# Expert gathers and their transposes apart, head norms of 1024 tokens at once, and a shorter inverse root

## The chip, the cores and the metric

The kernel runs on one core of a Trainium2 chip. Time is device time in microseconds (us) of one execution; the kernel before has a median of 3851.04 us over 3 runs (3839.18 to 3854.27). Engines are called by the profile's names: PE (TensorE; PEld its weight loads), DVE (VectorE), ACT (ScalarE), POOL (GpSimd), SP (SyncE, which issues most DMAs).

## The reference

One encoder layer on x of 2048 tokens by 1024 channels, in float32:

1. `h = rmsnorm(x) * (1 + sc1) + sh1`, then `p = h @ w_in`, which gives q, k, v for attention (8 query heads, 2 key/value heads of 64) and r, k, v and three low-rank inputs for RWKV-7 (8 heads of 64).
2. Attention: q and k are normalized per head, `y * rsqrt(mean(y*y) + 1e-6) * gain`, rotated, and go through a softmax over all 2048 tokens.
3. RWKV-7 in both directions. Its key `kk` is normalized per head too: `kk / max(sqrt(sum(kk*kk)), 1e-12)`. The output has a group norm per head.
4. `x = x + gt1 * (concat(o_att, o_rwkv) @ w_out)`.
5. Expert choice: `aff = softmax(h2 @ w_router)`; each of 16 experts takes its 256 best tokens, gathers their rows of h2 and computes `(silu(hg @ w_gate) * (hg @ w_up)) @ w_down`, scaled by the affinity, and adds the rows into the output.

## The kernel before, in words

The work is written in Tile: the program names tiles in pools (a tag with n buffers is a ring of n), and a planner orders each engine's instructions. It runs the program on a modelled timeline: when an engine is free there, it issues the earliest instruction of the program that is ready by the model. The order found so is fixed; on the chip each engine takes its own queue in order and waits at semaphores. An instruction can therefore stand in a queue long before its place in the program, and its wait on the chip holds up all behind it on that engine.

Float32 products are made of three single-pass products: each operand is split into a rounded half (ACT) and a remainder (DVE or POOL), `hi*hi + hi*lo + lo*hi` (`split`, L143).

**Projections** (`phase1`, from about 36 to 740 us). Two halves of 1024 tokens. In each, columns of `w_in` are taken 128 at a time (`load_w`, `project`, L245), over four pieces of 256 tokens. `ORDER` fixes the sequence of items: `h` a pair of rwkv heads (three column groups r, k, v, then `prep`), `q` a column group of queries (then `qk_post`), `v` the values, `x` an early load of tokens. Both `qk_post` and `prep` loop over two quarters `q` of 512 tokens and call `head_rsqrt` (L265) in each: ACT squares the tile, four small matmuls with `bones` sum the squares over the 64 rows of each head into PSUM tile `pn` (L272), ACT copies them (`hsm`), PE transposes (L275), DVE scales (`hss`, L280 or L282) and takes the inverse root in 128 x 8 (`rsqrt`, L49 to L61), and splits it into two halves in `rp` (L290, L291); PE transposes back (L292), ACT copies (`hrt`, L294) and four matmuls with `sel` spread the result over the rows again (`pb`, L297). DVE then multiplies it into the tile (`qk_xn` L311, `kkn` L364). `qk_post` also swaps neighbouring rows by two DMAs into `qk_sw`, which shares its one buffer with the squares `qk_sq`. That makes 36 calls of `head_rsqrt`: 2 halves x (5 + 4) column groups x 2 quarters.

The inverse root is a bit trick (L55: shift, L57: subtract from a constant) and three Newton steps of three instructions (L59 to L61), 11 instructions on DVE. The token loads (`load_x`), the group norm of the mixers and the output projection use it as well.

**Mixers** (740 to 2340 us): attention and the RWKV scan side by side. **Output projection** and affinities (2340 to 2590), **router** (2590 to 2657).

**Experts** (`moe`, 2657 to 3850). For each expert: for `f2` = 0 to 3, load and split 256 columns of `w_gate` and `w_up_e` (L1435, L1438); for each of the two column groups `f` of 128 in it, 48 matmuls `gu` (L1496), silu and product `hid` (L1499, L1500), and its split into `dh`, `dl`. Then 96 matmuls `down` (L1515), `y` (L1520), and two scatters that add into the output (POOL, L1521). After `f2` = 0, `choose(e + 1)` prepares the next expert: 16 one-hot tiles `oh` (L1450), 32 small list matmuls into PSUM tile `list_ps` (L1455), the row numbers `idx` (L1459), two gathers of 128 rows into `xg` (POOL, L1460), and at once 16 transposes `moe_tr` in four steps (L1472), each followed by scaling on DVE (`ht`, L1476) and a split into `hh`, `hl`. `list_ps` and `moe_tr` share the PSUM tag `x`, which has two buffers; `idx`, `xg`, `hh` and `hl` have two each.

Of the kernel before, what the change touches and what calls it, by code (L numbers as in the profile page):

```python
# [17 lines left out]
P = 128  # L18
# [19 lines left out]
class Encoder:  # L38
# [10 lines left out]
    def rsqrt(self, pool, y, x, n, pp=P):  # L49

        nc = self.nc
        t = pool.tile([P, n], F32, tag=f"rsq_t{n}", name="rsq_t")
        ti = t.bitcast(I32)
        xi = x.bitcast(I32)
        nc.vector.tensor_scalar(out=ti[:pp], in0=xi, scalar1=1, scalar2=None, op0=ALU.logical_shift_right)  # L55
        yi = y.bitcast(I32)
        nc.vector.tensor_scalar(out=yi, in0=ti[:pp], scalar1=-1.0, scalar2=float(0x5F3759DF), op0=ALU.mult, op1=ALU.add)  # L57
        for _ in range(3):
            nc.vector.tensor_tensor(out=t[:pp], in0=y, in1=y, op=ALU.mult)  # L59
            nc.vector.scalar_tensor_tensor(out=t[:pp], in0=t[:pp], scalar=-0.5, in1=x, op0=ALU.mult, op1=ALU.mult)  # L60
            nc.vector.scalar_tensor_tensor(out=y, in0=t[:pp], scalar=1.5, in1=y, op0=ALU.add, op1=ALU.mult)  # L61


    def params(self):
# [199 lines left out]

    def head_rsqrt(self, sq, scale, eps, floor, kind="n"):  # L265

        nc, tp = self.nc, self.tpool
        tag = kind + "_ps"
        pn = self.ps_n.tile([P, 4, P], F32, tag=tag, name="pn")

        for i in range(4):
            nc.tensor.matmul(pn[32 * i : 32 * i + 32, 0, :], self.bones, sq[:, i * P : (i + 1) * P], start=True, stop=True, tile_position=(0, 32 * i))  # L272
        sm = tp.tile([P, P], F32, tag="hsm", name="hsm")
        nc.scalar.copy(out=sm, in_=pn[:, 0, :])
        nc.tensor.transpose(pn[:, 1, :], sm, self.ident)  # L275
        pv = pn[:, 1, :].rearrange("p (i r) -> p i r", r=32)[:, :, 0:2]
        ss = tp.tile([P, 8], F32, tag="hss", name="hss", bufs=2)
        s3 = ss.rearrange("p (i h) -> p i h", h=2)
        if floor is None:
            nc.vector.tensor_scalar(out=s3, in0=pv, scalar1=scale, scalar2=eps, op0=ALU.mult, op1=ALU.add)  # L280
        else:
            nc.vector.tensor_scalar(out=s3, in0=pv, scalar1=floor, scalar2=None, op0=ALU.max)  # L282
        rn = tp.tile([P, 8], F32, tag="hrn", name="hrn", bufs=2)
        self.rsqrt(tp, rn, ss, 8)

        self.rpn += 1
        rp = self.rp[self.rpn % 2]
        r4 = rp.rearrange("p (i x) -> p i x", x=32)
        r3 = rn.rearrange("p (i h) -> p i h", h=2)
        nc.vector.tensor_copy(out=r4[:, :, 0:2], in_=r3)  # L290
        nc.vector.tensor_tensor(out=r4[:, :, 2:4], in0=r3, in1=r4[:, :, 0:2].bitcast(F32), op=ALU.subtract)  # L291
        nc.tensor.transpose(pn[:, 2, :], rp.bitcast(F32), self.ident)  # L292
        rt = tp.tile([P, P], F32R, tag="hrt", name="hrt")
        nc.scalar.copy(out=rt, in_=pn[:, 2, :])  # L294
        pb = self.ps_n.tile([P, 512], F32, tag=tag, name="pb")
        for i in range(4):
            nc.tensor.matmul(pb[:, i * P : (i + 1) * P], self.sel[:, i, :], rt, start=True, stop=True)  # L297
        return pb

    def qk_post(self, half, j, p, rope):  # L300

        nc = self.nc
        gain = self.qkn[:, 0:1] if j < 4 else self.qkn[:, 1:2]
        co, si = rope
        for q in range(2):
            qs = slice(q * 512, (q + 1) * 512)
            t0 = half * HT + q * 512
            sq, xn, t1, t2 = [self.tpool.tile([P, 512], F32, tag="qk_" + t, name="qk_" + t) for t in ("sq", "xn", "t1", "t2")]
            nc.scalar.activation(out=sq, in_=p[q], func=AF.Square)
            pb = self.head_rsqrt(sq, 1.0 / CH, 1e-6, None, "q")  # L310
            nc.vector.scalar_tensor_tensor(out=xn, in0=p[q], scalar=gain, in1=pb, op0=ALU.mult, op1=ALU.mult)  # L311
            sw = self.tpool.tile([P, 512], F32, tag="qk_sq", name="qk_sw")
            for i in range(2):
                nc.sync.dma_start(out=sw[i : P : 2, :], in_=xn[1 - i : P : 2, :])
            nc.gpsimd.tensor_tensor(out=t1, in0=xn, in1=co[:, qs], op=ALU.mult)
            nc.vector.tensor_tensor(out=t2, in0=sw, in1=si[:, qs], op=ALU.mult)
            nc.vector.tensor_tensor(out=t1, in0=t1, in1=t2, op=ALU.add)
            nc.sync.dma_start(out=self.d_qk[j, :, t0 : t0 + 512], in_=t1)
# [25 lines left out]
    def prep(self, half, ct, rkv, lora, rates, sg):  # L344
# [5 lines left out]
        c2 = lambda ap: ap.rearrange("p (c t) -> p c t", t=P)  # L350
        c3 = lambda ap: ap.rearrange("p (c t) -> p c t", t=CH)
        c4 = lambda ap: ap.rearrange("p (c u t) -> p c u t", u=2, t=CH)
        for q in range(2):
            qs = slice(q * 512, (q + 1) * 512)
            t0 = half * HT + q * 512
# [1 line left out]
            r, k, v = rkv[0][q], rkv[1][q], rkv[2][q]  # L357
            tl = lambda tag, bufs=None: tpool.tile([P, 512], F32, tag=tag, name=tag, bufs=bufs)
            self.to_tokens(v, self.d_v[t0 : t0 + 512, cs_])
            ksq = tl("ksq")  # L360
            act(out=ksq, in_=k, func=AF.Square, scale=self.kk[:, ct : ct + 1])
            pb = self.head_rsqrt(ksq, None, None, 1e-24)
# [59 lines left out]
    def phase1(self):  # L422
# [13 lines left out]
        with ExitStack() as c:  # L436
# [17 lines left out]
            self.rp = [self.tpool.tile([P, P], F32R, name=f"rp{i}") for i in range(2)]  # L454
            self.rpn = 0
            for t in self.rp:
                nc.vector.tensor_copy(out=t, in_=self.zero[:, 0:1].to_broadcast([P, P]))
# [737 lines left out]
class Ffn(Rwkv):  # L1195
# [217 lines left out]
    def moe(self, c):  # L1413
# [27 lines left out]
        def choose(e):  # L1441
# [21 lines left out]
            val = tp.tile([P, 2], F32, tag="val", name="val")  # L1463
            nc.vector.tensor_tensor(out=val, in0=lst[:, :, 3], in1=lst[:, :, 4], op=ALU.add)
            nc.vector.tensor_tensor(out=val, in0=val, in1=lst[:, :, 2], op=ALU.add)
            hh = tp.tile([P, KT, CAP], F32R, tag="hh", name="hh")
            hl = tp.tile([P, KT, CAP], F32R, tag="hl", name="hl")
            for k2 in range(4):
                pt = ps.tile([P, 2, CAP], F32, tag="x", name="moe_tr", bufs=2)
                for i in range(2):  # L1470
                    for h in range(2):
                        nc.tensor.transpose(pt[:, i, h * P : (h + 1) * P], xg[:, h, (2 * k2 + i) * P : (2 * k2 + i + 1) * P], self.ident)  # L1472
                ht = tp.tile([P, 2, CAP], F32, tag="ht", name="ht")
                for i in range(2):
# [4 lines left out]
            return idx, val, hh, hl  # L1479

        def expert(e, st):
            idx, val, hh, hl = st
            nxt = None
            dh = tp.tile([P, 8, CAP], F32R, tag="dh", name="dh", bufs=1)
            dl = tp.tile([P, 8, CAP], F32R, tag="dl", name="dl", bufs=1)
            for f2 in range(4):
# [3 lines left out]
                for i in range(2):  # L1490
                    f = 2 * f2 + i
                    acc = ps.tile([P, 2, CAP], F32, tag="gu", name="gu", bufs=2)
                    for m, (wh, wl) in enumerate((g, u)):
                        for kt in range(KT):
                            for n, (a, b) in enumerate(((wh, hh), (wh, hl), (wl, hh))):
                                nc.tensor.matmul(acc[:, m, :], a[:, kt, i * P : (i + 1) * P], b[:, kt, :],  # L1496
                                                 start=(kt == 0 and n == 0), stop=(kt == KT - 1 and n == 2))
                    hid = tp.tile([P, CAP], F32, tag="hid", name="hid")
                    nc.scalar.activation(out=hid, in_=acc[:, 0, :], func=AF.Silu)  # L1499
                    nc.vector.tensor_tensor(out=hid, in0=acc[:, 1, :], in1=hid, op=ALU.mult)  # L1500
                    self.split(dh[:, f, :], dl[:, f, :], hid)
                if f2 == 0 and e + 1 < NE:
                    nxt = choose(e + 1)
            po = [ps.tile([P, 512], F32, tag=f"d{i}", name="down") for i in range(4)]
            for f2 in range(4):
                w = weight(io["w_down"][0, e, f2 * 256 : (f2 + 1) * 256, :].rearrange("(k p) d -> p k d", p=P))
# [17 lines left out]

        self.listed = None
        st = choose(0)
        for e in range(NE):
            st = expert(e, st)

# [59 lines left out]
```

## Time and profile before

| | us |
|---|---|
| median of 3 runs | 3851.04 |
| profiled execution | 3852.07 |
| its span (first to last instruction) | 3850.1 |
| PE busy | 3546.8 (92%) |
| DVE busy | 2581.8 (67%) |
| ACT busy | 1758.1 (46%) |
| POOL busy | 1537.9 (40%) |

Busy time is the union of an engine's instructions. PE's matmuls are pipelined: one is shown for about 0.28 us, and the next starts 0.11 to 0.12 us after it. PEclk is the granted TensorE clock, 1.00 for 2.4 GHz.

### The profile page before, as it was taken

The numbers are of one execution on the slowest core, as the hardware profiler recorded it, in microseconds if no ns is written. First come the engines' busy times: TensorE is split into PE (matmuls) and PEld (weight loads), VectorE is DVE, ScalarE is ACT, GpSimd is POOL, SyncE is SP. The second block draws the span as 40 slices with busy tenths as digits, with TensorE's granted clock in tenths as the row PEclk, the third lists the DMA queues.
The fourth block names the chain that finished last, engine by engine and source line by source line (L and its number), as shares of the span: only waits on it lengthen the run. The fifth ranks groups of instructions, "written<-read, shape, count | busy, mean of one in ns | idle before, by whom it ended". The sixth has DMA issues, their size and how long they took to land. (4 is left out here: it accounts for less than half of the span.)

```text
span 3850.1 us, 61939 instructions
## 1 busy us (share of the span) xinstructions
PE 3546.8 (92%) x23436; PEld 2875.5 (75%) x23436; DVE 2581.8 (67%) x4704; ACT 1758.1 (46%) x3102; POOL 1537.9 (40%) x1484
## 2 busy tenths in 40 slices
PE   6997898899999999999999998994999999999998
PEld 5986888656666666766666665774888888888897
DVE  6689788886768677558867675457555556555653
ACT  4445444424555555645555663231434443443442
POOL 3344344436363443663363644323223323322331
PEclk8999999789999899999999999996999999999999
DMA  5235334443323433533233233442566667566664
GB/s 182 94 126 167 105 113 137 147 113 78 82 70 90 120 82 82 117 92 85 77 76 92 61 88 113 142 164 99 188 202 202 197 197 211 183 203 200 200 193 134
DMA packets 531230, 510.95 MB, mean 133 GB/s; under 512 B 213304, under 2 KB 449954, under 8 KB 525812
## 3 DMA queue, kind: packets, MB, share of 16 engines
q1 hardware_dynamic: 520612, 472.08, 40.4%
q0 software_dynamic: 10000, 34.91, 4.0%
q8 instruction: 185, 3.03, 0.3%
q14 instruction: 113, 0.93, 0.1%
q10 hardware_dynamic: 320, 0.00, 0.0%
HBM read 392.57 MB, written 109.07 MB: 130 GB/s over the span
## 5 line engine op out<-in xcount | busy, mean ns | idle before, releaser
L1438 DVE TENSOR_TENSOR w_lo<-w_raw,w_hi 128x2048 fp32r<-128x2048 f32 x189 | 462.2, 2451 | 339.2 <-ACT w_hi L1435 339.1
L1496 PE MATMUL gu<-hh,w_hi 128*128 128x256 f32 x2048 | 578.9, 283 | 0.1
L1496 PE MATMUL gu<-hh,w_lo 128*128 128x256 f32 x2048 | 577.4, 282 | 0.0
L1496 PE MATMUL gu<-hl,w_hi 128*128 128x256 f32 x2048 | 575.1, 281 | 0.0
L685 POOL TENSOR_TENSOR acc<-acc,pt 128x512 f32<-128x512 f32 x256 | 363.3, 1424 | 454.8 <-ACT pt L682 433.4
L1435 ACT CAST w_hi<-w_raw 128x2048 fp32r<-128x2048 f32 x192 | 366.8, 1912 | 316.8 <-PE gu L1496 146.1
L682 ACT ACTIVATE pt<-st_ps 128x1024 f32<-128x1024 f32 x256 | 262.2, 1024 | 404.2 <-PE st_ps L681 231.4
L635 DVE TENSOR_REDUCE mx<-s_ps 128x1 f32<-128x512 f32 x512 | 343.3, 681 | 152.8 <-PE s_ps L634 151.0
L245 PE MATMUL proj_ps<-hh,w_hi 128*128 128x258 f32 (+1 forms) x1280 | 375.9, 294 | 28.3 <-DVE s_k L263 12.9
L1496 PEld LDWEIGHTS gu<-hh,w_hi 128*128 128x128 f32 x2048 | 390.1, 191 | 1.6 <-DVE hid L1500 0.2
L1496 PEld LDWEIGHTS gu<-hl,w_hi 128*128 128x128 f32 x2048 | 390.3, 191 | 1.3
L1496 PEld LDWEIGHTS gu<-hh,w_lo 128*128 128x128 f32 x2048 | 390.9, 191 | 0.0
L245 PE MATMUL proj_ps<-hl,w_hi 128*128 128x258 f32 (+1 forms) x1280 | 373.4, 292 | 3.3 <-DVE hl L147 2.5
L245 PE MATMUL proj_ps<-hh,w_lo 128*128 128x258 f32 (+1 forms) x1280 | 372.6, 292 | 0.7 <-POOL w_lo L147 0.7
L147 POOL TENSOR_TENSOR dl<-hid,dh 128x256 fp32r<-128x256 f32 x128 | 139.3, 1089 | 390.1 <-ACT dh L146 389.7
L672 PE MATMUL o_ps<-pt,av 128*64 128x512 f32 x1024 | 279.8, 626 | 6.7 <-ACT pt L682 6.7
L245 PEld LDWEIGHTS proj_ps<-hh,w_hi 128*128 128x128 f32 x1280 | 250.6, 196 | 37.4 <-issue 28.7
L685 DVE TENSOR_TENSOR acc<-acc,pt 128x512 f32<-128x512 f32 x192 | 185.4, 966 | 111.2 <-ACT pt L682 110.6
L245 PEld LDWEIGHTS proj_ps<-hl,w_hi 128*128 128x128 f32 x1280 | 251.3, 196 | 7.3 <-DVE hl L147 2.9
L633 PE MATMUL s_ps<-khh,qhl 128*128 128x512 f32 x512 | 241.5, 473 | 14.7 <-DVE mx L635 12.8
L245 PEld LDWEIGHTS proj_ps<-hh,w_lo 128*128 128x128 f32 x1280 | 250.4, 196 | 4.5 <-issue 2.3
L680 PE MATMUL st_ps<-qhl,khh 128*128 128x512 f32 x512 | 229.1, 447 | 2.6 <-ACT pt L682 2.6
(410 smaller groups left out, 8255.4 us busy)
## 6 DMA issues: line engine op xcount, KB each, us to landing
w_raw<-in_w_gate_dram SPq DMA_DIRECT2D x64, 1024.0 KB
w_raw<-in_w_up_e_dram SPq DMA_DIRECT2D x64, 1024.0 KB
w_raw<-in_w_down_dram SPq DMA_DIRECT2D x64, 1024.0 KB
d_x<-X SPq DMA_DIRECT2D x32, 1024.0 KB
xin<-d_x SPq DMA_DIRECT2D x64, 512.0 KB
w_raw<-in_w_in_dram SPq DMA_DIRECT2D x80, 256.0 KB
mod_w<-in_w_ada_dram SPq DMA_DIRECT2D x64, 256.0 KB
mod_w<-in_w_ada_dram SPq DMA_DIRECT2D x8, 1024.0 KB
```

What stands on the lines that cost most here:

```text
L147: (eng or nc.gpsimd).tensor_tensor(out=lo, in0=src, in1=hi.bitcast(F32), op=ALU.subtract)
L245: nc.tensor.matmul(acc[:, :n], a[:, kt, :], b[:, kt, lo : lo + n], start=(kt == 0 and m == 0), stop=(kt == KT - 1 and m == 2))
L633: nc.tensor.matmul(s, qs[h][:, ts], khh[:, ks], start=True, stop=False)
L635: nc.vector.tensor_reduce(out=mx[:, 4 * h + qt, kc : kc + 1], in_=s, axis=AX.X, op=ALU.max)
L672: nc.tensor.matmul(av[64 * h : 64 * h + 64, :], v[:, kb, :], pt[:, h, :], start=(kb == 0), stop=(kb == 15), tile_position=(0, 64 * h))
L680: nc.tensor.matmul(s[:, h, :], khh[:, ks], qs[h], start=True, stop=False)
L682: nc.scalar.activation(out=pt, in_=s, func=AF.Exp, scale=0.125)
L685: eng.tensor_tensor(out=acc[:, h, :], in0=(first if kb == 1 else acc)[:, h, :], in1=pt[:, h, :], op=ALU.add)
L1435: nc.scalar.copy(out=hi, in_=raw)
L1438: eng.tensor_tensor(out=lo, in0=raw, in1=hi.bitcast(F32), op=ALU.subtract)
L1496: nc.tensor.matmul(acc[:, m, :], a[:, kt, i * P : (i + 1) * P], b[:, kt, :], start=(kt == 0 and n == 0), stop=(kt == KT - 1 and n == 2))
```

## The change

- `rsqrt` computes the same function with 8 instructions. The first makes the start value in one (the integer multiplied by -0.5 and added to the constant), then one step of higher order and one Newton step, with constants folded in.
- `head_rsqrt` takes the squares of 1024 tokens (both quarters) in one tile. The numbers of matmuls and transposes per 512 tokens stay; the copies and the DVE instructions are made once for both quarters, on 16 columns instead of 8. The spreading is a function of its own, `spread`, called per quarter.
- `qk_post` and `prep` square both quarters ahead of their loop. The squares of both have one tag, `sq`, with one buffer of 2 x 512 columns; the swapped tile of `qk_post` is written into it. `hsm` and `hrt` share the tag `hsm`, with one buffer. `rp` has one tile instead of two.
- In `moe`, `choose` ends after the gathers. The transposes are a generator, `fetch`, of four steps; one step stands after each column group of `f2` = 2 and 3.

```diff
     def rsqrt(self, pool, y, x, n, pp=P):
...
+        nc.vector.tensor_scalar(out=y.bitcast(I32), in0=x.bitcast(I32), scalar1=-0.5, scalar2=float(0x5F3759DF), op0=ALU.mult, op1=ALU.add)
+        tt(out=t, in0=y, in1=y, op=ALU.mult)
+        tt(out=t, in0=t, in1=x, op=ALU.mult)
+        stt(out=t, in0=t, scalar=-10.0 / 3.0, in1=t, op0=ALU.add, op1=ALU.mult)
+        stt(out=y, in0=t, scalar=5.0, in1=y, op0=ALU.add, op1=ALU.mult)
+        tt(out=t, in0=y, in1=y, op=ALU.mult)
+        stt(out=t, in0=t, scalar=-0.5 * 0.375**3, in1=x, op0=ALU.mult, op1=ALU.mult)
+        stt(out=y, in0=t, scalar=1.5 * 0.375, in1=y, op0=ALU.add, op1=ALU.mult)
...
     def head_rsqrt(self, sq, scale, eps, floor, kind="n"):
+        pn = self.ps_n.tile([P, 4, P], F32, tag=kind + "_ps", name="pn")
+        for q in range(2):
+            for i in range(4):
+                nc.tensor.matmul(pn[32 * i : 32 * i + 32, q, :], self.bones, sq[:, q, i * P : (i + 1) * P], start=True, stop=True, tile_position=(0, 32 * i))
+        sm = tp.tile([P, 2, P], F32, tag="hsm", name="hsm")
+        nc.scalar.copy(out=sm, in_=pn[:, 0:2, :])
+        for q in range(2):
+            nc.tensor.transpose(pn[:, 2 + q, :], sm[:, q, :], self.ident)
...
+        for q in range(2):
+            nc.tensor.transpose(pn[:, q, :], rp[:, q, :].bitcast(F32), self.ident)
+        rt = tp.tile([P, 2, P], F32R, tag="hsm", name="hrt")
+        nc.scalar.copy(out=rt, in_=pn[:, 0:2, :])
+        return rt
+
+    def spread(self, rt, q, kind="n"):
+        pb = self.ps_n.tile([P, 512], F32, tag=kind + "_ps", name="pb")
         for i in range(4):
-            nc.tensor.matmul(pb[:, i * P : (i + 1) * P], self.sel[:, i, :], rt, start=True, stop=True)
+            self.nc.tensor.matmul(pb[:, i * P : (i + 1) * P], self.sel[:, i, :], rt[:, q, :], start=True, stop=True)
         return pb
...
     def prep(self, half, ct, rkv, lora, rates, sg):
+        ksq = tpool.tile([P, 2, 512], F32, tag="sq", name="ksq")
+        for q in range(2):
+            act(out=ksq[:, q, :], in_=rkv[1][q], func=AF.Square, scale=self.kk[:, ct : ct + 1])
+        rt = self.head_rsqrt(ksq, None, None, 1e-24)
         for q in range(2):
...
+            pb = self.spread(rt, q)
...
         def choose(e):
...
+            return [idx, val, xg]
+
+        def fetch(st):
+            xg = st[2]
             hh = tp.tile([P, KT, CAP], F32R, tag="hh", name="hh")
             hl = tp.tile([P, KT, CAP], F32R, tag="hl", name="hl")
+            st[2:] = hh, hl
             for k2 in range(4):
...
+                yield
 
         def expert(e, st):
...
+                    if f2 >= 2:
+                        next(steps, None)
                 if f2 == 0 and e + 1 < NE:
                     nxt = choose(e + 1)
+                    steps = fetch(nxt)
```

## Rows read from the trace of the kernel before

**Rows 1.** The page's first part: busy us, share of the span, instructions.
```profile
PE 3546.8 (92%) x23436; PEld 2875.5 (75%) x23436; DVE 2581.8 (67%) x4704; ACT 1758.1 (46%) x3102; POOL 1537.9 (40%) x1484
```

**Rows 2.** Busy time by stage: stretch, length, busy of PE, PEld, DVE, ACT, POOL, PEclk.
```profile
140.00:740.00 600.00, 528.34 (x4000) 483.49 (x3998) 510.49 (x1085) 292.46 (x625) 260.77 (x188) 0.95 0.39 129
2657.00:3767.00 1110.00, 1054.84 (x7928) 984.77 (x7927) 636.76 (x796) 463.48 (x484) 328.54 (x242) 0.99 0.63 197
...
3030.00:3104.00 74.00, 69.81 (x530) 64.98 (x530) 43.04 (x55) 30.83 (x32) 22.64 (x16) 1.00 0.64 200
3767.00:3834.00 67.00, 67.00 (x481) 63.05 (x480) 29.15 (x24) 24.96 (x26) 11.94 (x11) 1.00 0.42 126
```

**Rows 3.** PE's waits, 2660 to 3850 us: total us, times, longest.
```profile
PE moe_tr L1472 <- DMA xg<-d_xh,idx: 41.1, 23, 4.5
PE list_ps L1455 <- DVE ht L1476: 13.9, 11, 1.3
```

**Rows 4.** PE's waits in the projections, 140 to 740 us.
```profile
PE pbo L410 <- DVE pinv L408: 15.1, 6, 4.8
PE proj_ps L245 <- DVE s_k L263: 12.9, 5, 3.9
...
PE proj_ps L245 <- DVE s_r L263: 6.3, 3, 2.8
PE pn L292 <- DVE rp L291: 5.8, 6, 2.6
PE pn L272 <- ACT qk_sq L309: 5.3, 4, 3.4
PE proj_ps L245 <- DVE s_v L263: 4.0, 2, 3.4
PE pn L272 <- DVE kkn L364: 2.9, 4, 1.9
```

**Rows 5.** PE's timeline in the sixth expert: start, duration, instruction, [idle before].
```profile
3030.28 0.28 PE L1496 MATMUL gu<-hh,w_hi 128*128 128x256 f32 x1
...
3046.53 0.30 PE L1472 MATMUL moe_tr<-ident,xg 128*128 128x128 f32 x1 [1.81 <-DMA xg<-d_xh,idx]
...
3054.64 0.88 PE L1472 MATMUL moe_tr<-ident,xg 128*128 128x128 f32 x6 [1.08 <-DMA xg<-d_xh,idx]
...
3064.65 0.56 PE L1455 MATMUL list_ps<-parts,oh 128*128 128x5 bf16 x16 [1.30 <-DVE ht L1476]
```

**Rows 6.** POOL's timeline in the same expert.
```profile
3039.81 1.00 POOL L1460 DMA_INDIRECT xg<-d_xh,idx  x1 [0.30 <-issue]
...
3044.63 3.04 POOL L1460 DMA_INDIRECT xg<-d_xh,idx  x1 [0.92 <-DVE oh L1450]
...
3056.95 1.30 POOL L147 TENSOR_TENSOR hl<-ht,hh 128x512 fp32r<-128x512 f32 x1 [4.63 <-ACT hh L146]
```

**Rows 7.** DVE by line, 0 to 830 us: count, busy us, mean ns, idle before.
```profile
L59 DVE TENSOR_TENSOR rsq_t<-hrn 128x8 f32<-128x8 f32 x108 | 32.8, 304 | 2.3
...
L60 DVE SCALAR_TENSOR_TENSOR rsq_t<-rsq_t,hss 128x8 f32<-128x8 f32 x108 | 25.7, 238 | 2.4
L61 DVE SCALAR_TENSOR_TENSOR hrn<-rsq_t,hrn 128x8 f32<-128x8 f32 x108 | 25.6, 237 | 2.3
...
L55 DVE TENSOR_SCALAR rsq_t<-hss 128x8 int32<-128x8 int32 x36 | 14.5, 403 | 0.4
L57 DVE TENSOR_SCALAR hrn<-rsq_t 128x8 int32<-128x8 int32 x36 | 13.5, 376 | 0.4
```

**Rows 8.** Line 59 alone: ns min/median/max, first and last start, forms.
```profile
L59 DVE TENSOR_TENSOR rsq_t<-hrn x108: 141/166/1286, 72.4 to 775.5; 128x8 f32<-128x8 f32 x108
...
L59 DVE TENSOR_TENSOR rsq_t<-gn_m x33: 129/161/2258, 1187.9 to 2343.9; 128x16 f32<-128x16 f32 x21, 128x4 f32<-128x4 f32 x12
```

**Rows 9.** ACT's timeline at the head of one norm's chain.
```profile
421.25 0.63 ACT L309 ACTIVATE qk_sq<-p 128x512 f32<-128x512 f32 x1 [0.95 <-DVE qk_t L316]
```

**Rows 10.** PE's timeline at the end of the same chain.
```profile
434.86 0.56 PE L297 MATMUL pb<-hrt,sel 128*128 128x128 f32 x4
```

More of the change, by code (lines that the diff above doesn't have):

```diff
@@ L51, in rsqrt @@
         nc = self.nc
[L52 to L61, printed above, removed]
+        t = pool.tile([P, n], F32, tag=f"rsq_t{n}", name="rsq_t")[:pp]
+        tt, stt = nc.vector.tensor_tensor, nc.vector.scalar_tensor_tensor
+        nc.vector.tensor_scalar(out=y.bitcast(I32), in0=x.bitcast(I32), scalar1=-0.5, scalar2=float(0x5F3759DF), op0=ALU.mult, op1=ALU.add)
[6 more added lines that the diff above has]
+        stt(out=y, in0=t, scalar=1.5 * 0.375, in1=y, op0=ALU.add, op1=ALU.mult)
     def params(self):
@@ L267, in head_rsqrt @@
         nc, tp = self.nc, self.tpool
[L268 to L277, printed above, removed]
+        pn = self.ps_n.tile([P, 4, P], F32, tag=kind + "_ps", name="pn")
[6 more added lines that the diff above has]
+            nc.tensor.transpose(pn[:, 2 + q, :], sm[:, q, :], self.ident)
+        pv = pn[:, 2:4, :].rearrange("p q (i r) -> p (q i) r", r=32)[:, :, 0:2]
+        ss = tp.tile([P, 16], F32, tag="hss", name="hss", bufs=2)
         s3 = ss.rearrange("p (i h) -> p i h", h=2)
@@ L282, in head_rsqrt @@
             nc.vector.tensor_scalar(out=s3, in0=pv, scalar1=floor, scalar2=None, op0=ALU.max)
-        rn = tp.tile([P, 8], F32, tag="hrn", name="hrn", bufs=2)
-        self.rsqrt(tp, rn, ss, 8)
+        rn = tp.tile([P, 16], F32, tag="hrn", name="hrn", bufs=2)
+        self.rsqrt(tp, rn, ss, 16)
         self.rpn += 1
-        rp = self.rp[self.rpn % 2]
-        r4 = rp.rearrange("p (i x) -> p i x", x=32)
+        rp = self.rp[self.rpn % len(self.rp)]
+        r4 = rp.rearrange("p q (i x) -> p (q i) x", x=32)
         r3 = rn.rearrange("p (i h) -> p i h", h=2)
@@ L291, in head_rsqrt @@
         nc.vector.tensor_tensor(out=r4[:, :, 2:4], in0=r3, in1=r4[:, :, 0:2].bitcast(F32), op=ALU.subtract)
[L292 to L295, printed above, removed]
+        for q in range(2):
[5 more added lines that the diff above has]
+        pb = self.ps_n.tile([P, 512], F32, tag=kind + "_ps", name="pb")
         for i in range(4):
-            nc.tensor.matmul(pb[:, i * P : (i + 1) * P], self.sel[:, i, :], rt, start=True, stop=True)
+            self.nc.tensor.matmul(pb[:, i * P : (i + 1) * P], self.sel[:, i, :], rt[:, q, :], start=True, stop=True)
         return pb
@@ L304, in qk_post @@
         co, si = rope
+        sq = self.tpool.tile([P, 2, 512], F32, tag="sq", name="qk_sq")
+        for q in range(2):
+            nc.scalar.activation(out=sq[:, q, :], in_=p[q], func=AF.Square)
+        rt = self.head_rsqrt(sq, 1.0 / CH, 1e-6, None, "q")
         for q in range(2):
@@ L307, in qk_post @@
             t0 = half * HT + q * 512
-            sq, xn, t1, t2 = [self.tpool.tile([P, 512], F32, tag="qk_" + t, name="qk_" + t) for t in ("sq", "xn", "t1", "t2")]
-            nc.scalar.activation(out=sq, in_=p[q], func=AF.Square)
-            pb = self.head_rsqrt(sq, 1.0 / CH, 1e-6, None, "q")
+            xn, t1, t2 = [self.tpool.tile([P, 512], F32, tag="qk_" + t, name="qk_" + t) for t in ("xn", "t1", "t2")]
+            sw = sq[:, q, :]
+            pb = self.spread(rt, q, "q")
             nc.vector.scalar_tensor_tensor(out=xn, in0=p[q], scalar=gain, in1=pb, op0=ALU.mult, op1=ALU.mult)
-            sw = self.tpool.tile([P, 512], F32, tag="qk_sq", name="qk_sw")
             for i in range(2):
@@ L352, in prep @@
         c4 = lambda ap: ap.rearrange("p (c u t) -> p c u t", u=2, t=CH)
+        ksq = tpool.tile([P, 2, 512], F32, tag="sq", name="ksq")
+        for q in range(2):
+            act(out=ksq[:, q, :], in_=rkv[1][q], func=AF.Square, scale=self.kk[:, ct : ct + 1])
+        rt = self.head_rsqrt(ksq, None, None, 1e-24)
         for q in range(2):
@@ L359, in prep @@
             self.to_tokens(v, self.d_v[t0 : t0 + 512, cs_])
-            ksq = tl("ksq")
-            act(out=ksq, in_=k, func=AF.Square, scale=self.kk[:, ct : ct + 1])
-            pb = self.head_rsqrt(ksq, None, None, 1e-24)
+            pb = self.spread(rt, q)
             kk = tl("kkn", 2)
@@ L453, in phase1 @@
                 nc.vector.memset(self.bones[64 * h : 64 * h + 64, h : h + 1], 1.0)
-            self.rp = [self.tpool.tile([P, P], F32R, name=f"rp{i}") for i in range(2)]
+            self.rp = [self.tpool.tile([P, 2, P], F32R, name=f"rp{i}") for i in range(1)]
             self.rpn = 0
             for t in self.rp:
-                nc.vector.tensor_copy(out=t, in_=self.zero[:, 0:1].to_broadcast([P, P]))
+                nc.vector.tensor_copy(out=t, in_=self.zero[:, 0:1].unsqueeze(2).to_broadcast([P, 2, P]))
             self.sel = self.tpool.tile([P, 4, P], F32R, name="sel")
@@ L1478, in choose @@
                 self.split(hh[:, 2 * k2 : 2 * k2 + 2, :], hl[:, 2 * k2 : 2 * k2 + 2, :], ht)
-            return idx, val, hh, hl
+                yield
         def expert(e, st):
             idx, val, hh, hl = st
-            nxt = None
+            nxt, steps = None, iter(())
             dh = tp.tile([P, 8, CAP], F32R, tag="dh", name="dh", bufs=1)
@@ L1526, in moe @@
         st = choose(0)
+        for _ in fetch(st):
+            pass
         for e in range(NE):
```

## The prediction

> **What bounds the kernel now.** I read the page's busy shares first: TensorE is busy 92% of the span, VectorE 67%, ScalarE 46%, GpSimd 40% [rows 1]. The table of stages comes next, because the change touches only some of them [rows 2]. It shows the projections (140 to 740 us; the first 140 us are the start) with TensorE busy 528 of 600 us and VectorE 510, so two engines are nearly full there; and fifteen of the sixteen experts (2657 to 3767 us) with TensorE busy 1055 of 1110 and VectorE at 637, so TensorE alone sets the pace. The mixers between them and the output projection run the edited inverse root a few times only. So what can be won is TensorE's idle time: 72 us in the projections, 55 us in the experts. The third view, the waits of TensorE, names what ends it. In the experts there are only two causes: 41.1 us in 23 waits of the transposes `moe_tr` for the gathered rows `xg`, and 13.9 us in 11 waits of the list matmuls for VectorE's `ht` [rows 3]. In the projections the causes are many and small, and most are VectorE's [rows 4].
>
> An expert without a successor has none of this: the sixteenth takes 67 us with TensorE busy throughout, while the sixth, which chooses the seventh, takes 74 with 69.8 busy [rows 2].
>
> **Experts: the waits for the gathers.** The transposes stand in TensorE's queue at the place where the planner thinks that the rows have landed, and TensorE takes its queue in order. In the sixth expert, which starts at 3030.28, the first transpose comes at 3046.53 after 1.81 us of idleness and the next six at 3054.64 after 1.08 us, both ended by the DMA [rows 5]. The two gathers were issued at 3039.81 and 3044.63 [rows 6], so the second half of the rows is there 24.4 us after the expert's start.
>
> Where does the change put the first transposes? Behind the fifth of eight column groups. The sixteenth expert gives the pitch: 384 narrow matmuls and 96 of double width in 67.0 us are 576 units of 0.116 us, so a group of 48 takes 5.6 us and five take 28 [rows 2]. 28 is later than 24.4, by 3.6 us, and each further step of four transposes comes 5.6 us later. If the queue keeps this order, the 41.1 us go almost whole. What is late next is the list matmuls' wait: they take a PSUM buffer that a transpose's reader `ht` has to free. Today eight transposes come nearly together and their readers stand behind weight splits on VectorE; the sixth expert loses 1.30 us there [rows 5]. With steps 5.6 us apart the buffer should mostly be free, but the next list can also land behind another weight split, so I take half: 7 us of 13.9, between nothing and all of it.
>
> What the move carries with it: per expert 16 transposes, 8 VectorE scalings, 4 ScalarE copies and 4 GpSimd subtractions of 1.3 us each [rows 6]. None is added; all run some 12 us later. VectorE has 31 of 74 us free in an expert, ScalarE 43, GpSimd 51 [rows 2]. The last step is issued after the eighth group, at about 46 us, and its result is needed at the next expert's start, behind 96 down matmuls (22 us); if that cover were gone the next expert's first matmuls would wait. The gathers themselves and the scatters ahead of them on GpSimd's queue keep their places; the four subtractions now come before the next scatter, which waits for the down matmuls anyway. SP's weight loads are not passed. So this part gives 41 + 7 = 48 us; the bounds are 0 (the planner pulls the transposes forward again) and 61 (all 55 us, and some 6 of the 11 us that a granted clock of 0.99 over 1110 us costs [rows 2]).
>
> **Projections: norms of 1024 tokens at once.** There are 36 calls of the norm now and 18 after. Each call's inverse root is 11 VectorE instructions now and 8 after: 396 become 144, so 252 go. In the trace the 396 took 32.8 + 25.7 + 25.6 + 14.5 + 13.5 = 112 us, 283 ns each [rows 7]. Their median is 166 ns for 8 columns, and 161 for the 16-column form that the group norm uses [rows 8], so the doubled width is free. Saved on VectorE: 252 x 0.166 = 42 us at the least, 252 x 0.283 = 71 us at the most. Three smaller instructions around each root (scale, copy, subtract) go with the 18 calls too; I leave them as a margin. TensorE's work stays: the same four sums, one transpose there, one back and four spreads for each 512 tokens. ScalarE's two copies become half as many, twice as wide, which costs nothing on an engine that is half idle in this stage [rows 2].
>
> Here a rule speaks against the upper figure. The rows show single small instructions far above their median (up to 1.29 us) [rows 8]. The Trainium skill, page "SBUF — State Buffer", section "SBUF: two separate sides", says that VectorE and GpSimd lock a shared port pair for a whole instruction and that the other engine blocks fully. By it a stall behind GpSimd does not vanish with the instruction that met it but falls on the next one with two SBUF inputs; the saving would then be the 42 us and not the 71. The long single instructions agree with it; that a stall is passed on, no row of before shows.
>
> How much of 42 to 71 us reaches the end? TensorE's waits for VectorE here are 15.1 + 12.9 + 6.3 + 5.8 + 4.0 + 2.9 = 47 us [rows 4]. Between none and all of that I take a bit over a third, 18 us: VectorE's load of 510 us falls by about a tenth, and the waits for the chain's own steps (`rp`, `kkn`, 8.7 us together) occur half as often.
>
> What is added is a dependency. The first 512 tokens' normalized tile now waits for the sums of all 1024. In program order it costs little, since the projections of r, k and v of a head are all issued before its norms. But `sq` and `hsm` have one buffer each and are now shared by the q/k norms and the rwkv norms; `hsm` holds the result until the second half has been spread. Behind a late `hsm` copy, ScalarE's evictions of the projections would queue, and behind these TensorE's accumulators. That is a rival below. Against it stands one gain that I don't price: the second half's Square today waits for the swapped tile of the first half to be read [rows 9], and no longer does.
>
> **Inverse root elsewhere.** The output projection and the group norm lose 3 small instructions per call beside a busier TensorE. Only the start (first x tile) and the last token tile before the router lie open: 2 x 3 x 0.17 = 1 us. Bounds 0 and 3. The order of the mixers is planned anew, since everything before them moves; I allow 10 us either way.
>
> **Sum.** 48 + 18 + 1 = 67 us, from the profiled execution's 3852.1 us (span 3850.1 and 2 us around it): 3785. That execution lies 1 us above the median of the three runs, 3851.0, so nothing is to be corrected.
>
> **The rivals.**
> - *The planner undoes the move.* List matmuls of the eighth expert, which stand in the program after a quarter of the seventh, run at 3064.65, in the middle of the sixth [rows 5]. So the planner fills what it takes for idle time with later work, and could issue the transposes as early as before. For: that row. Against: they now stand behind all of groups three to five in priority, and those are ready whenever their weights are. The experts give 5 us or so, the rest as above: 3852 - 5 - 18 - 1 = 3828.
> - *Waits for gathers go, the projections give nothing.* VectorE's 42 us end up as its own idle time because the waits are for chains across engines. 3852 - 48 = 3804.
> - *Both give more.* 61 in the experts and 40 of the 47 in the projections: 3751.
> - *Slower: the joint norms lie bare.* One chain from Square to spread lasts 421.25 to 434.86, 13.6 us [rows 9, 10]. If a third of the 18 joint chains stood bare because of the single `hsm` or `sq` buffer, TensorE would lose 6 x 13.6 = 82 us: 3852 - 49 + 82 = 3885. The total turns slower when four of 18 are bare (54 us against 49). Against it: today the waits for the chain's own steps (5.3 + 5.8 + 2.9 = 14 us, [rows 4]) are 3% of 36 chains of 13.6 us; they are well covered by projections.
>
> **How the numbers follow.** Forecast 45%; projections give nothing 25%; planner undoes the move 13%; both give more 10%; slower 7%. The range 3742 to 3830 takes in the forecast, both smaller gains and most of the larger one, and leaves out the slower case. What this kernel's measurement can tell from no change is about 0.5%, 19 us: faster means below 3832, slower above 3870. Faster: nearly all of the first two and of "more", about half of the third, 80%. Same: the rest of the third, and mishaps of the planner's new order in the others, 13%. Slower 7%.
>
> **What would show it.** Experts: the wait of `moe_tr` for `xg` near 0 in the table of TensorE's waits, and an expert at about 70.5 us instead of 74. Still 30 us or more there: the planner pulled them forward. List waits: at or below 7 us; above 14, the PSUM buffer is the new bound. Projections: 18 norms, VectorE busy 40 to 70 us less between 140 and 740 us, the stage about 18 us shorter. A stage that is not shorter although VectorE is less busy speaks for the second case; new waits of TensorE for `hsm` or the sums, or of ScalarE for them, for the slower one. The prediction is wrong if the experts' part stays within 20 us of before, or if the projections get longer.

## The result, and the profile after

The changed kernel takes 3744.51 us (median of 4 runs, 3741.77 to 3751.49) against 3846.84 us for the kernel before on the same chips (3839.18 to 3854.27): a ratio of 0.9737, 95% interval 0.9711 to 0.9762, about 102 us less. The forecast was 67 us less (3785, range 3742 to 3830). The profiled execution took 3751.5 us, 7 above its median, as the one of before stood some 5 above the median that more runs gave it.

Stages, from the first start of a mixer matmul (`p`), of the output projection, of the first `gu`, and the end of the last `down` in the two traces:

| us | start and projections | mixers | output projection, router | experts |
|---|---|---|---|---|
| before | 739 | 1597 | 322 | 1177 |
| after | 724 | 1576 | 326 | 1108 |
| difference | -15 | -21 | +4 | -69 |

The page's first line after the change; it answers to [rows 1].

```profile
PE 3509.9 (94%) x23436; PEld 2856.7 (76%) x23436; DVE 2516.7 (67%) x4289; ACT 1755.2 (47%) x3066; POOL 1512.5 (40%) x1484
```

Busy time by stage after, with the columns of [rows 2]: projections, mixers, the experts with a successor, the sixth of them, the sixteenth.

```profile
140.00:724.00 584.00, 521.18 (x3968) 479.80 (x3966) 475.87 (x789) 289.49 (x595) 265.76 (x188) 0.94 0.39 133
724.00:2300.00 1576.00, 1515.03 (x8963) 1047.22 (x8964) 1142.01 (x1913) 838.00 (x1666) 768.43 (x859) 0.96 0.36 90
2626.00:3668.00 1042.00, 1042.00 (x7923) 978.61 (x7923) 617.81 (x795) 464.09 (x483) 306.30 (x242) 1.00 0.66 209
2974.00:3044.00 70.00, 70.00 (x532) 65.67 (x531) 42.13 (x55) 30.88 (x32) 20.28 (x16) 1.00 0.67 211
3668.00:3734.00 66.00, 66.00 (x483) 61.80 (x482) 29.65 (x24) 25.00 (x26) 12.14 (x11) 1.00 0.43 128
```

In the experts TensorE is busy 1042 of 1042 us at a granted clock of 1.00, where it was 1055 of 1110 at 0.99. Both waits of [rows 3] are gone: the table of TensorE's waits has no row at all between 2626 and 3749 us. The transposes of the sixth expert (which starts at 2974.55) on TensorE's timeline, to be laid beside [rows 5]; no idle time stands behind them. They run in two bursts of eight, 26.3 and 38.4 us after the start, and not in four steps of four:

```profile
3000.80 1.03 PE L1492 MATMUL moe_tr<-ident,xg 128*128 128x128 f32 x8
3012.98 1.03 PE L1492 MATMUL moe_tr<-ident,xg 128*128 128x128 f32 x8
```

And its gathers on GpSimd's timeline, beside [rows 6]:

```profile
2987.64 3.04 POOL L1474 DMA_INDIRECT xg<-d_xh,idx  x1 [3.32 <-DVE idx L1473]
2990.98 1.07 POOL L1474 DMA_INDIRECT xg<-d_xh,idx  x1 [0.30 <-issue]
```

They go out 13.1 and 16.4 us after the expert's start and not 9.5 and 14.4 as before. The list matmuls ahead of them moved too: before, sixteen of them ran half an expert early (34 us into the expert ahead, [rows 5]), now nearly all run 11 and 15 us into the expert in which the program has them:

```profile
2985.45 0.53 PE L1469 MATMUL list_ps<-parts,oh 128*128 128x5 bf16 x15
2989.58 0.56 PE L1469 MATMUL list_ps<-parts,oh 128*128 128x5 bf16 x16
```

I read the reason from the trace: the last transposes hold the two PSUM buffers until 39 us into the expert, so the next list is no longer pulled so far ahead. The second gather lands 23.3 us after the expert's start (24.3 before), 3.0 us ahead of the first transposes.

### The profile page after: what moved, and what is told of

It reads as the page before. It is cut to its first block, busy times and chain, and to the rows that moved or that the text cites. A ratio compares the mean times of both kernels' runs of the same rounds, so it can differ in the third digit from the quotient of the medians.

```text
span 3749.8 us, 61495 instructions
## 1 busy us (share of the span) xinstructions
PE 3509.9 (94%) x23436; PEld 2856.7 (76%) x23436; DVE 2516.7 (67%) x4289; ACT 1755.2 (47%) x3066; POOL 1512.5 (40%) x1484
## 3 DMA queue, kind: packets, MB, share of 16 engines
q1 hardware_dynamic: 520612, 472.08, 41.1%
## 5 line engine op out<-in xcount | busy, mean ns | idle before, releaser
L1452 DVE TENSOR_TENSOR w_lo<-w_raw,w_hi 128x2048 fp32r<-128x2048 f32 x189 | 432.3, 2293 | 385.8 <-ACT w_hi L1449 385.4
L699 POOL TENSOR_TENSOR acc<-acc,pt 128x512 f32<-128x512 f32 x256 | 354.9, 1391 | 469.0 <-ACT pt L696 456.0
L696 ACT ACTIVATE pt<-st_ps 128x1024 f32<-128x1024 f32 x256 | 262.2, 1024 | 394.8 <-PE st_ps L695 221.2
L699 DVE TENSOR_TENSOR acc<-acc,pt 128x512 f32<-128x512 f32 x192 | 194.7, 1014 | 91.0 <-ACT pt L696 90.3
```

Of the source, the lines that this page charges most:

```text
L696: nc.scalar.activation(out=pt, in_=s, func=AF.Exp, scale=0.125)
L699: eng.tensor_tensor(out=acc[:, h, :], in0=(first if kb == 1 else acc)[:, h, :], in1=pt[:, h, :], op=ALU.add)
L1452: eng.tensor_tensor(out=lo, in0=raw, in1=hi.bitcast(F32), op=ALU.subtract)
```

## The experiments

Medians against the kernel before, run beside each; stages from the profiles as above.

| run | ratio (95%) | start and projections | mixers | out, router | experts |
|---|---|---|---|---|---|
| changed_again | 0.9757 (0.9730 to 0.9784) | 724 | 1574 | 325 | 1108 |
| experts_only | 0.9818 (0.9796 to 0.9841) | 734 | 1583 | 320 | 1108 |
| norms_root | 0.9901 (0.9876 to 0.9926) | 722 | 1578 | 325 | 1173 |
| norms_only | 1.0016 (0.9994 to 1.0038) | 737 | 1607 | 321 | 1168 |
| root_only | 1.0024 (1.0007 to 1.0041) | 732 | 1595 | 325 | 1173 |
| tokens_later | 0.9918 (0.9892 to 0.9943) | 722 | 1572 | 325 | 1178 |
| old_root_heads | 0.9870 (0.9816 to 0.9924) | 733 | 1619 | 325 | 1108 |
| spare_three | 0.9758 (0.9702 to 0.9814) | 720 | 1573 | 325 | 1109 |
| old_root_after | 0.9775 (0.9734 to 0.9816) | 722 | 1600 | 321 | 1108 |
| old_root_after_again | 0.9775 (0.9750 to 0.9800) | 722 | 1601 | 320 | 1107 |
| steps_early | 0.9811 (0.9765 to 0.9858) | 720 | 1582 | 324 | 1122 |
| steps_burst | 0.9803 (0.9758 to 0.9848) | 724 | 1587 | 325 | 1121 |

**The four parts.** Each part of the diff alone, or two together; no other edit.

> The kernel before with the change in the experts alone; projections, mixers and output projection keep their old order. Theory (the experts' gain is the waits of TensorE for gathers and list buffers, 55 us, plus the clock that these waits cost, some 10): 65 to 70 us faster than before, every expert that has a successor at 69 to 70 us, and the mixers unchanged within 5 us, with the stretches of half clock near 1284 and 1345 us there again. Rival A (the 21 us in the mixers differ from execution to execution): the mixers are about 20 us shorter here too, 85 to 90 us in all. Rival B (the experts gain only beside the rest of the change, for instance because their weights start earlier): below 50 us.

70 us faster, experts 1177 to 1108, no wait of TensorE in them. The gain is the theory's, B is refuted; the mixers were to stay within 5 us and did not. A holds in part: the order of TensorE, ScalarE and GpSimd ahead of the experts is that of before, and yet the mixers of this execution are 14 us shorter than those of the execution of before. The stretch of half clock near 1284 us, which the theory expected again, is not there: the granted clock from 1280 to 1320 us is 0.91, and was 0.62 before. First before, then experts_only:

```profile
739.00:2336.00 1597.00, 1533.41 (x8975) 1056.53 (x8974) 1145.51 (x1961) 842.69 (x1675) 777.90 (x861) 0.95 0.36 90
```

```profile
734.00:2317.00 1583.00, 1518.96 (x8974) 1047.97 (x8975) 1149.51 (x1961) 841.35 (x1675) 779.74 (x860) 0.96 0.36 90
```

TensorE's idle time is the same (64 us); the granted clock is not. So a difference of some 15 us in one pair of profiles of the mixers proves nothing. The -15 and -21 us of the first table are -10 and -7 if experts_only, which has before's order there, stands for before.

> The kernel before with the inverse root of 8 instructions alone, 36 calls as before. Theory (an inverse root is hidden work; it takes 108 VectorE instructions out of the projections, 18 to 31 us of VectorE's time there, and some 5 of it reach TensorE): projections 0 to 8 us shorter, the mixers anywhere within 20 us either way because they are planned anew, in all 0 to 25 us faster. Rival C (the mixers gain 21 us because their group norms' roots are shorter): mixers 15 to 25 us shorter, with VectorE's waits there shorter and not the clock. Rival D (the roots' length sets the projections): projections 12 us shorter or more by this alone.

> The kernel before with the norms of 1024 tokens at once, but the old inverse root of 11 instructions, and the old experts. Theory (half as many chains is what the projections gain from): projections 8 to 14 us shorter than before, VectorE busy some 50 us less between 140 and 740 us; mixers planned anew, within 20 us either way. Rival D (the root's length sets the projections): projections 0 to 4 us shorter. Rival E (the single buffers for the squares and the copies cost what the fewer chains give): projections not shorter, with new waits for hsm.

> The changed kernel with the old experts; everything ahead of the experts stands as in the changed kernel. Theory: 30 to 36 us faster than before, of which 12 to 15 in the projections and about 20 in the mixers, with less half clock between 1280 and 1360 us than before; with the experts' 65 to 70 us it makes up the whole 102. Rival A (the mixers' part differs from execution to execution): 12 to 16 us faster only. Rival F (part of the experts' gain comes through the parts ahead of them): the two parts do not add up to 102, by more than 10 us.

Neither norms nor root gains anything alone; both are slightly slower if anything (norms +6 us, root +9 us, by the ratios). Together they gain 38 us (28 to 48). With the experts' 70 that is 108, and the whole was measured at 101 and 93 by its two ratios: the parts add up within their intervals. How the 38 divide between projections and mixers single profiles don't settle. D falls with root_only, whose projections are 7 us shorter and not 12. E falls in its simple form: TensorE waits for `hsm` 1.9 us in all in norms_only. My own theories fall too. root_only was to be up to 25 us faster; and norms_only has 198 VectorE instructions fewer than before in the roots alone (36 x 11 against 18 x 11), VectorE is busy 481 us in its projections and not 510, and they are not shorter (737) than before's 734 to 739.

**Load, length or order?** Three edits on the changed kernel ask which of them matters. The old root in the head norms alone:

```diff
-        self.rsqrt(tp, rn, ss, 16)
+        self.rsqrt_old(tp, rn, ss, 16)
```

> The changed kernel with the old root of 11 instructions in the 18 joint head norms alone, 54 VectorE instructions more in the projections than the changed kernel; the new root everywhere else. Theory (the joint norms win in the projections only together with the shorter root, through the order that the planner then finds): projections 592 to 600 us instead of 584, the mixers as in the changed kernel, in all 10 to 20 us slower than it, about 3760. Rival C (the shorter roots of the group norms are what the mixers gain from): mixers near 1577 us too; so the mixers decide between C and a mere by-product of the projections' plan, under which they are at 1590 or more and the whole at 3770 to 3785. Rival J (VectorE's load alone counts): 54 instructions of 0.17 to 0.28 us are 9 to 15 us of VectorE's time, at its 80% load 2 to 5 us in all, about 3748.

The same 54 instructions more, but beside the chain:

```diff
         self.rsqrt(tp, rn, ss, 16)
+        for _ in range(3):
+            spare = tp.tile([P, 16], F32, tag="hss", name="spare", bufs=2)
+            nc.vector.tensor_tensor(out=spare, in0=self.sparein[:, 0:16], in1=self.sparein[:, 0:16], op=ALU.mult)
...
+            self.sparein = self.tpool.tile([P, 16], F32, name="sparein")
+            nc.vector.memset(self.sparein, 1.0)
```

> The changed kernel with three more small VectorE instructions (128 x 16, on tiles that nothing needs) beside each of the 18 joint head norms, off its chain: the load of the old root without its latency. Theory (the order that the planner finds, and not the load or the chain's length, makes the difference): a new order, and a time that may lie anywhere between that of the changed kernel and 20 us more. Rival J (VectorE's load): within 6 us of the run with the old root in the heads. Rival K (the length of the chain): within 5 us of the changed kernel, projections 580 to 586 us.

Beside the chain the load costs nothing that can be told: spare_three's ratio is 0.9758, the changed kernel's 0.9737 and 0.9757. The same load inside the chain costs 47 us (medians 3800 against 3753, run beside each other); in the profiles, of which spare_three's lies 9 us below its median, 13 us of the difference lie in the projections and 46 in the mixers, where these norms run only in the first 16 us. Projections and mixers of spare_three, then of old_root_heads:

```profile
140.00:720.00 580.00, 521.69 (x3965) 480.98 (x3963) 473.39 (x834) 289.24 (x593) 263.77 (x188) 0.94 0.39 134
720.00:2293.00 1573.00, 1511.03 (x8966) 1041.91 (x8966) 1142.92 (x1917) 841.57 (x1670) 772.65 (x860) 0.96 0.36 91
```

```profile
140.00:733.00 593.00, 524.33 (x3969) 480.24 (x3969) 475.92 (x840) 288.92 (x591) 260.98 (x188) 0.95 0.38 131
733.00:2352.00 1619.00, 1541.80 (x8966) 1061.13 (x8966) 1140.06 (x1914) 840.30 (x1670) 774.92 (x860) 0.94 0.35 88
```

VectorE is busy as long in both, so J falls. In the mixers both run the same number of matmuls; what differs is their sequence. Compared by name, TensorE's sequence in the mixers is the changed kernel's in spare_three, without one difference; in old_root_heads it differs in over 200 places. norms_only runs nearly the sequence of old_root_heads there (27 places differ) and takes 1607 us. So the longer mixers come with the other order that the planner finds once the chain in the projections is longer. How much of the 46 us that order causes is open: TensorE's idle time accounts for 15, and the lower granted clock for some 28 (an estimate from the length and the mean clock of the two stretches, 0.943 against 0.959). Before and experts_only show that some 15 of such clock can come and go under one order.

The rest of the forecasts did less well. For old_root_heads the whole (3800) lies above both that it named, 3760 and 3770 to 3785. In spare_three the new order that my theory awaited hardly came (25 places of TensorE's in the projections, none in the mixers); rival K's forecast for the projections, 580 to 586, came true with 580. In the projections, then, the chain's length and the order that comes with it are not told apart.

The old root where the head norms are not:

```diff
-        self.rsqrt(self.r_p, st, sv, 2 * nt)
+        self.rsqrt_old(self.r_p, st, sv, 2 * nt)
...
-                self.rsqrt(tp, rs, ss[:, 0:1], 1)
+                self.rsqrt_old(tp, rs, ss[:, 0:1], 1)
```

> The changed kernel with the old root of 11 instructions in the group norms of the mixers and in the output projection, the new one in the projections. Theory (the mixers' gain is a by-product of the new plan and of the clock, not of shorter roots there): the same as the changed kernel within 12 us, mixers within 10 us of 1576. Rival C (the shorter roots of the group norms are it): mixers 15 to 25 us longer, 1590 to 1600 us.

> The changed kernel itself, beside the next run on one chip, so that the two can be compared; nothing is edited. Expected: 0.974 of the time of before, about 3745 us, mixers 1570 to 1590 us.

> The changed kernel with the old root in the group norms and the output projection, once more, because its first interval overlapped that of the changed kernel; the mixers' order on all engines is that of the changed kernel up to 1971 us, with 14 differences on TensorE after it. Theory (under one order the length of the group norms' roots is worth little): within 8 us of the run beside it. Rival C (the shorter roots of the group norms are a good part of the mixers' gain): 12 to 25 us slower than the run beside it, mixers 1590 to 1605 us.

The mixers are 1600 and 1601 us long in the two profiles, where C had them, against 1572 to 1587 in the seven others with the new root and the joint norms, all of which run one TensorE order there; the output projection is 4 us shorter. But both profiled executions were the slowest of their runs, 6 and 14 us above the median. The medians of the second comparison are 3753.9 against 3743.6, between the two forecasts (within 8, 12 to 25), and the intervals overlap. Rival C is neither confirmed nor refuted: by my estimate from these numbers 0 to 20 us of the mixers may go with the group norms' roots, though root_only has these roots too and no shorter mixers (1595). It stays open.

An edit that was to make a new order did not:

```diff
-            self.to_tokens(v, self.d_v[t0 : t0 + 512, cs_])
             pb = self.spread(rt, q)
             kk = tl("kkn", 2)
             stt(out=kk, in0=k, scalar=self.kkh[:, ct : ct + 1], in1=pb, op0=ALU.mult, op1=ALU.mult)
+            self.to_tokens(v, self.d_v[t0 : t0 + 512, cs_])
```

> The changed kernel with the old experts (as the run norms_root), in which the transposes and the store of v stand behind the key's product instead of ahead of the spread: the same instructions, another order in the program. Theory (norms and root together win 36 us partly because their plan happens to leave less half clock and fewer late instructions): the time differs from norms_root by more than its scatter, by 8 to 30 us, most of it in the projections and mixers. Rival I (the 36 us belong to the 306 instructions that are gone from VectorE): within 6 us of norms_root.

It is 6 us from norms_root. But TensorE's sequence in the projections and in the mixers is the same as there, so this run tells the two expectations apart in nothing.

**Where the transposes stand.** Two edits of the place, on the changed kernel:

```diff
-                    if f2 >= 2:
+                    if 2 <= f < 6:
                         next(steps, None)
```

> The changed kernel with the four steps of transposes behind the third to sixth column group instead of the fifth to eighth. Theory (what the move wins is that the transposes stand behind the landing of the gathers, which is about 24 us after an expert's start in both kernels): the third group ends near 17 us, so TensorE waits for the second half of the rows again, 2 to 7 us in each of 15 experts, and the stage of the experts is 30 to 80 us longer than in the changed kernel. Rival G (the win is the spreading over four places, wherever they are): the experts as fast as in the changed kernel, within 10 us. Rival H (the planner decides where they stand, and the place in the program matters little): within 10 us too, with the transposes still issued at 26 us or later.

```diff
-                    if f2 >= 2:
-                        next(steps, None)
+                    if f == 4:
+                        for _ in steps:
+                            pass
```

> The changed kernel with all four steps together behind the fifth column group. Theory (late is what counts; spreading only keeps the list matmuls from waiting for a PSUM buffer): no wait for the gathers, at most 1.3 us per expert for a buffer, so the experts 0 to 20 us longer than in the changed kernel. Rival G (spreading is what counts): 30 us longer or more.

TensorE's waits over the experts, steps_early and then steps_burst:

```profile
PE moe_tr L1492 <- DMA xg<-d_xh,idx: 13.1, 8, 2.2
```

```profile
PE moe_tr L1492 <- DMA xg<-d_xh,idx: 17.6, 14, 2.1
PE moe_tr L1492 <- DVE ht L1496: 0.5, 1, 0.5
```

Both are 13 to 14 us slower in the experts, and in both the wait for the gathers is back in part. For steps_early that is less than the 30 us of the theory and more than the 10 of rivals G and H: all three missed. Its gathers go out 13.1 and 16.4 us into the sixth expert (start 2981.2) as in the changed kernel, but its first transpose is due before the first of them has landed:

```profile
3003.67 0.30 PE L1492 MATMUL moe_tr<-ident,xg 128*128 128x128 f32 x1 [1.48 <-DMA xg<-d_xh,idx]
```

For steps_burst the theory's 0 to 20 us holds and G's 30 falls, though there was to be no wait for the gathers. steps_burst shows the rival of the prediction at work: the program places the first transpose behind the fifth group, and it is issued in the third, 16 us into the sixth expert (start 2986.7):

```profile
3002.68 0.30 PE L1492 MATMUL moe_tr<-ident,xg 128*128 128x128 f32 x1 [1.43 <-DMA xg<-d_xh,idx]
...
3013.86 0.82 PE L1492 MATMUL moe_tr<-ident,xg 128*128 128x128 f32 x6
3018.84 0.60 PE L1492 MATMUL moe_tr<-ident,xg 128*128 128x128 f32 x4
```

So place alone does not hold them back. With steps spread to the eighth group, the PSUM buffers are taken longer, list and gathers follow later, and the planner, which issues a transpose when its model takes the rows for landed, does so at 26 us. That the buffers are the link is read from the traces and was not tried by itself.

## Why the prediction was right, and where not

- *Waits for the gathers, 41 us:* right; they went whole, and experts_only shows that this edit alone does it. The margin was right (3.6 us forecast, 3.0 in the sixth expert), the way to it in part luck: the queue did not keep the program's order (two bursts at 26.3 and 38.4 us and not four steps from 28 us on), and the gathers, which were to keep their places, went out 2 to 4 us later. The rival of the undone move did not come true in this kernel, but does in part in steps_burst.
- *List buffers, 7 of 13.9 us:* undersized; all went. With the clock (about 23 us at half clock in the experts before, 3 after: some 10 us) that makes 41.1 + 13.9 + 10 = 65 of the 69 us measured, where the prediction had 48 and an upper bound of 61. Of the rest, 1.5 us is the sixteenth expert's (last section); some 2 are not assigned.
- *Projections, 18 us:* 15 measured in this pair of profiles, 10 against experts_only, and for a wrong reason. TensorE's idle time up to the first mixer matmul falls by 8 us (101 and 102 in the two executions of before's order, 94 and 93 in the two of the changed kernel); the rest is matmul time, and experts_only, with before's order, has 6 us less of that too, at a higher granted clock. The step that failed is "VectorE's load of 510 us falls by about a tenth, and the waits for the chain's own steps (`rp`, `kkn`, 8.7 us together) occur half as often", as a reason for 18 us. The chain's own waits did shrink (8.7 to 3.0 us), but the accumulators' waits grew from 23 to 25 us (`s_k`, `s_r`, `s_v`, [rows 4]), and all waits for VectorE together fell only from 52 to 48. norms_only and spare_three show that VectorE's load alone decides nothing here: with 29 us less of it the stage was 2 us shorter, 54 instructions more beside the chain did not lengthen it. TensorE's waits in the projections after:

```profile
PE proj_ps L247 <- DVE s_k L265: 23.8, 8, 4.8
PE pbo L424 <- DVE pinv L422: 7.9, 7, 2.7
...
PE pn L297 <- DVE rp L295: 1.1, 3, 0.6
...
PE proj_ps L247 <- DVE s_v L265: 0.8, 2, 0.6
```

- *The saving on VectorE, 42 to 71 us:* right for the roots, wrong for the engine. The head norms' roots took 112 us in 396 instructions before [rows 7] and take 53 us in 144 after, 59 less. That is under the upper figure because those left are slower each, 367 ns on average against 283, with medians almost as before (164 to 176 ns by line against 166). The small instructions around the roots fell too, from 24 to 11 us. Yet VectorE's busy time between 140 us and the first mixer matmul fell from 510 to 476 only, 34 us, which is below the lower end. Most of the difference was taken up by the 304 instructions of `prep`, which are the same in both kernels and rose from 285 to 311 us; the rest is not assigned. Three lines of the roots (VectorE by line, 0 to 830 us, the columns of [rows 7]), then one line of `prep` before and after:

```profile
L56 DVE TENSOR_TENSOR rsq_t<-hrn 128x16 f32<-128x16 f32 x18 | 8.6, 479 | 0.6
L61 DVE TENSOR_TENSOR rsq_t<-hrn 128x16 f32<-128x16 f32 x18 | 7.5, 414 | 0.1
L55 DVE TENSOR_SCALAR hrn<-hss 128x16 int32<-128x16 int32 x18 | 7.4, 411 | 0.4
```

```profile
L399 DVE SCALAR_TENSOR_TENSOR a<-a,kkn 128x512 f32<-128x512 f32 x32 | 30.6, 957 | 0.7 <-ACT kd L398 0.3
```

```profile
L413 DVE SCALAR_TENSOR_TENSOR a<-a,kkn 128x512 f32<-128x512 f32 x32 | 40.4, 1261 | 0.0
```

  The longest root instruction after shows a stall: on VectorE's timeline it lasts 4.63 us and ends with the second of two subtractions in a row on GpSimd, the first of which began before it (GpSimd's timeline below). By the Trainium skill, "SBUF — State Buffer", section "SBUF: two separate sides", the engine that holds the shared port pair keeps it for a whole instruction and the other blocks fully; this row agrees. That such stalls pass to other instructions when some are taken away is what I worked out from it: the rows of `prep` agree, but no run shows the cause of each.

```profile
729.51 4.63 DVE L61 TENSOR_TENSOR rsq_t<-hrn 128x16 f32<-128x16 f32 x1
```

```profile
728.91 5.20 POOL L614 TENSOR_TENSOR kl<-k_raw,khh 64x1024 fp32r<-64x1024 f32 x2
```

  One reading of the prediction was loose: the 161 ns for 16 columns [rows 8] is a median over two forms, of 16 and of 4 columns. The doubled width is nearly free all the same, by the medians above.
- *Mixers, 0 with 10 us either way:* too small. The kernels with joint norms and new root have 1572 to 1587 us there; the two executions of before's order 1583 and 1597; old_root_heads 1619. One order can thus be some 30 to 45 us longer than another in a profile, the clock's part included.
- *Output projection, -1 us:* it is 4 us longer in every kernel with the new root there (324 to 326) than in those with the old (320 to 322); the reason was not looked for.
- *The joint norms and the shorter root as two gains:* the prediction counts them together on VectorE's load. Alone each gained nothing (norms +6 us, root +9), together 38; why they gain only together stays open between the chain's length and the planner's order.
- *Slower by bare chains:* no. TensorE's waits for `hsm` after are 5 us in all. A second buffer for `hsm` was not tried.

## What to carry to other kernels

A wait that recurs at one place of an otherwise full engine's queue is the safest thing to take away; add to its price the waits queued behind the same buffers and the clock that it costs. Where a planner orders the work, an edit also brings a new order, and that can outweigh what it saves: test an edit's parts alone and together, and test load by putting the removed instructions back off the chain. An engine's busy time is not the sum of fixed prices: here roots of 59 us went, and the busy time fell by 34. Compare a stage between kernels only beyond what two executions of one order differ by.

## What the runs showed of the hardware

The `gu` matmuls have two steady pitches at granted clock 1.00, in the same kernel and expert: 0.113 us (24 matmuls from 2977.28 to 2980.00) and 0.118 us (24 from 2992.08 to 2994.90). Long stretches keep one of them. The sixteenth expert ran mostly at the slow one before (67 us) and at the fast one after (66 us), with the same matmuls. What selects it was not found.

```profile
2977.28 0.28 PE L1516 MATMUL gu<-hh,w_hi 128*128 128x256 f32 x1
...
2980.00 0.28 PE L1516 MATMUL gu<-hh,w_hi 128*128 128x256 f32 x1
```

```profile
2992.08 0.28 PE L1516 MATMUL gu<-hh,w_hi 128*128 128x256 f32 x1
...
2994.90 0.28 PE L1516 MATMUL gu<-hh,w_hi 128*128 128x256 f32 x1
```

VectorE's busy time in the stage of the projections repeats far better than its length when the order is the same: 593.3 and 593.4 us up to the first mixer matmul in the two executions of before's order, while the stage took 739 and 734 us. TensorE's idle time there repeats too (101 and 102 us); what differs is the granted clock, 0.933 and 0.946 on average over the stage.
